# Reordering the first stage, and the last gate pair with its neighbours, in a one-core hybrid decoder step

## The chip, the cores and the metric

The kernel runs on one core of one Trainium2 chip. The metric is the device time of one execution in microseconds. Engine names are those of the profile: PE is TensorE, DVE is VectorE, ACT is ScalarE, POOL is GpSimd, SP is the engine that issues most DMAs. Each engine runs its own instructions strictly in order, and so does SP's queue of DMA issues: what waits for a semaphore holds everything behind it.

## The reference

One layer is computed for a prompt of 1024 tokens with 16 meta tokens ahead of it, and for 8 single sample tokens. All matrices are float32.

```
xn = rmsnorm(h, norm_pre);  proj = xn @ w_in                  # 1024 -> 10 sections of 1024
q, fr, i_in, z_a, b_g, c_g, h_c, z_b, gate_a, gate_b = split(proj)
f = lb + (1 - lb) * sigmoid(fr);  k = 1 - f;  q = silu(q)
o_t = q_t^T S_t,   S_t = diag(f_t) S_{t-1} + k_t v_t^T        # per head, 8 heads of 128 x 128
y_a = (rmsnorm(o) * silu(z_a)) @ w_a
u = c_g * h_c;  y_b = (b_g * conv3(u) * silu(z_b)) @ w_b
out = (sigmoid(gate_a) * y_a + sigmoid(gate_b) * y_b) @ w_o
h = h + rmsnorm(out, norm_post)
```

It also returns the recurrent state and the last two convolution rows for the prompt and the samples.

## The kernel before, in words

Each product of float32 numbers is made of three products of a cheaper type: a value is split into a high part (a cast on ACT) and a low part (value minus high part, a subtraction on DVE or POOL), and `mm3` (lines 114 to 116) multiplies high by high, high by low and low by high. A "product" below is one such PE instruction.

The token axis is cut into two halves of 524 columns (512 prompt tokens and 12 small ones), and each half into two pieces C0 (256 columns) and C1 (268). The program has these stages.

**First stage** (lines 980 to 1126). Eight chunks of 128 tokens are loaded: chunks 0, 2, 4, 6 by SP, chunks 1, 3, 5, 7 by an indirect DMA on POOL (line 167). Their tiles are u, a, s, ee, kt, v, x, zs in that order. For each chunk `square` takes the mean square on ACT (line 176) and its reciprocal root on POOL (lines 82 and 83, tile st), `normalise` scales it on DVE (line 183), `turns` transposes it on PE in two halves of four (line 192), `highs` casts on ACT (line 196) and `lows` subtracts on DVE (line 200). `plain` then multiplies the first two weight tiles, wi (tiles s4h, s4l, into psum ga) and wf (s5h, s5l, into psum gb), with four blocks of the tokens: s0 and s1 are chunks of the first half, s3 and s6 of the second; the weights' parts come from `w_high` on ACT and `w_low`. In all there are 8 such blocks of 24 products. `sums12` (line 219 on DVE, two per chunk pair) and `sums34` (line 219 on POOL) form sums of blocks, and some of these are transposed again: they feed the next stage.

**The Strassen stream.** `strassen` multiplies pairs of weight tiles by the block sums s0 to s6, with 7 instead of 8 block products. A pair has 14 steps: j = 0 to 6, for C0 and C1, with 12 products in each. In each step the weights for two steps later are split (line 605 on ACT, 611 on DVE or POOL), the results of the step before are taken out (`after`; line 570 copies j = 0, 2, 4 into a tile sc on ACT, two buffers; line 288 adds psum and sc on DVE), and then the `hooks` of that step run: a table from step number to side work (`at_step`). A0 is the first step of the pairs that multiply w_a, B0 = A0 + 56 that of w_b. The last pair ahead of A0 is a gate pair, for channels 6 and 7 of gate_b.

**Around A0.** `gate_pair` (line 749) takes a sigmoid of each result piece and stores it, 8 pieces of 128 by 256 or 260, to gb in memory; half of the pieces are stored out of the sc tile itself. `exchange` loads rows of the mixer's output into tiles u, v, a, kt, it (line 877) and splits them into new parts s0 to s6 (ACT line 90, DVE or POOL line 91), in steps A0-13 to A0+9. `block_sums` (line 840) loads two whole rows of the convolution branch, makes four sums of them on DVE (line 219) and stores them (lines 853 to 857): 12 steps each. `gates_in` loads two whole gate tiles of branch A for one pair of y (line 899); `y_pair` multiplies by them on DVE (line 911). `context_out` transposes and stores the convolution context. After the w_b pairs comes the output projection.

Of the kernel before, what the change touches and what calls it, by code (L numbers as in the profile page):

```python
# [20 lines left out]
HY = 516  # L21
# [11 lines left out]
def hybrid_step(ctx: ExitStack, tc: tile.TileContext,  # L33
# [26 lines left out]
    def slot(tag, n=NX, dt=F32):  # L60
        return sb.tile([128, n], dt, name=tag, tag=tag, bufs=BUFS.get(tag, 1))
# [46 lines left out]
    def sec_of(sec, m):  # L108
        c0 = 1024 * sec + 128 * m
        return w_in[0][:, c0:c0 + 128]  # L110
# [35 lines left out]
    def chunks_of(n):  # L146
        return (0, 256), (256, n - 256)
# [55 lines left out]
    def turns(c):  # L203
        for kk in range(2):
            turn(c, kk)
# [78 lines left out]
    def added(pt, s, out=None):  # L284
        if s is None:
            return pt
        out = s if out is None else out
        vec.tensor_tensor(out=out, in0=pt, in1=s, op=ALU.add)  # L288
        return out
# [459 lines left out]

    def gate_pair(sec, m, dst):  # L750
        def evac(r, h, c0, n, pt, s):
            y = added(pt, s)

            def gate():
                out = slot("cs", HL - 256)[:, 0:n] if s is None else s
                sigmoid(y, n, out)
                sync.dma_start(dst[m + r][:, HY * h + c0:HY * h + c0 + n], out)
            then(gate)

        return (sec_of(sec, m), sec_of(sec, m + 1)), chunks_of(HY), (), evac, lambda: None, factors  # L760

# [100 lines left out]
    def at_step(g, f):  # L862
        hooks.setdefault(g, []).append(f)
# [84 lines left out]

    gates = [gate_pair(8, m, ga_d) for m in (0, 2, 4, 6)] + [gate_pair(9, m, gb_d) for m in (0, 2, 4, 6)]
    stream_of = [head_pairs(0)[1]]  # L950
# [11 lines left out]
    exchange(B0 - 26, B0 - 14, sets_b, ob_d, *sums_b, ("kt", "x", "zs"))  # L962
    at_step(A0 + 18, lambda: context_out())

    def at_steps(g, side):
        for i in range(12):
            at_step(g + i, lambda: next(side, None))
# [3 lines left out]
    for k in range(4):  # L971
        at_steps(S0 + int(15.75 * (k + 5)) + 5, block_sums(k, oz_d, *sums_a, ("f", "k", "s")))
        at_steps((A0 - 52, A0 - 40, A0 - 28, A0 + 2)[k], block_sums(k, ob_d, *sums_b, ("f", "k", "s") if k < 3 else ("x", "zs", "x")))
    for i, m in enumerate((0, 2, 4, 6)):
        at_step(A0 - 11 + 14 * i, lambda m=m: gates_in(m))
        at_step(B0 - (4 if i else 11) + 14 * i, lambda m=m: gates_in_b(m))
# [5 lines left out]
    load_chunk(0)  # L982
    load_chunk(1)
    load_chunk(3)
    sync.dma_start(wpre, norm_pre.broadcast_to([128, 1024]))
# [9 lines left out]
    load_chunk(6)  # L995
    load_small()
    wi, wf = (tuple(p[:, 0:1024] for p in t) for t in (t3, t4))
# [4 lines left out]
    def w_low(r, w, kk):  # L1002
        ks = slice(512 * kk, 512 * kk + 512)
        pool.tensor_tensor(out=w[1][:, ks], in0=r[kk], in1=w[0][:, ks].bitcast(F32), op=ALU.subtract)

    def plain(w, h, c0, n):
# [6 lines left out]
        return lambda: (i_out if w is wi else f_out)(0, h, c0, n, pt, None)  # L1013

    square(0)
    load_chunk(5)
    load_chunk(7)
    square(2)
    normalise(0)
    turns(0)  # L1020
    normalise(2)
    highs(0)
    square(1)
    lows(0)
    turns(2)
    for kk in range(2):
        w_high(ri, wi, kk)
        w_low(ri, wi, kk)
    highs(2)
    normalise(1)  # L1030
    lows(2)
    square(3)
    for kk in range(2):
        w_high(rf, wf, kk)
        w_low(rf, wf, kk)
    e1 = plain(wi, 0, *C0)
    turns(1)
    normalise(3)
    highs(1)
    lows(1)  # L1040
    square(4)
    turns(3)
    normalise(4)
    square(6)
    highs(3)
    lows(3)
    e2 = plain(wf, 0, *C0)
    turns(4)
    normalise(6)
    e1()  # L1050
    highs(4)
# [20 lines left out]
    vec.tensor_scalar(out=omlb, in0=lb, scalar1=-1.0, scalar2=1.0, op0=ALU.mult, op1=ALU.add)  # L1072
    square("s", 24)
    e1 = plain(wi, 1, *C0)
    turns(6)
    normalise("s", 24)
    highs(6)
    lows(6)
    square(5)
    square(7)  # L1080
    e2()
    flush()
    e2 = plain(wf, 1, *C0)
    normalise(5)
    s11, s12, s21, s22 = turn_small()
    for b, to in ((s11, b11), (s12, b12), (s21, b21), (s22, b22)):
        small_parts(b, to)
    normalise(7)
    turns(5)
    e1()  # L1090
    highs(5)
    lows(5)
    e1 = plain(wi, 0, *C1)
    turns(7)
    for out, a, b in ((s12, s12, s11), (s22, s22, s12), (s11, s22, s11), (s21, s21, s22)):
        less(out, a, b, vec)
    small_parts(s22, t2)
    e2()
    flush()
    highs(7)  # L1100
    lows(7)
    for i in range(2):
        sums12(i)
    e2 = plain(wf, 0, *C1)
    turn(1, 1)
    turn(3, 1)
    for i in range(2, 4):
        sums12(i)
    next(stream)
    for c in (1, 3):  # L1110
        turn_high(c, 1, t2)
        turn_low(c, 1, t2)
    e1()
    for i in range(4):
        sums34(i)
    e1 = plain(wi, 1, *C1)
    e2()
    flush()
    turn(5, 1)
    turn(7, 1)  # L1120
    e2 = plain(wf, 1, *C1)
    for c in (5, 7):
# [158 lines left out]
```

## Time and profile before

| what | value |
|---|---|
| time, median of 3 runs | 1298.46 us (1297.31 to 1299.75) |
| time of the profiled execution | 1297.85 us |
| its span, first to last instruction | 1296.1 us |
| PE busy | 1242.4 us, 96% of the span |
| DVE busy | 950.1 us, 73% |
| ACT busy | 581.8 us, 45% |
| POOL busy | 458.1 us, 35% |
| moved by DMA | 140.41 MB, mean 108 GB/s |
| mean granted clock of PE | 0.990 |

The time of the profiled execution is 1.75 us more than its span. The page cuts the span into 40 slices of 32.4 us. PE is at 9 tenths or more in nearly all of them; it is at 6 and 8 in the first two, at 8 in the slices from 875, 1004 and 1102 us, and at 7 in the last. So the places where PE waits are few, and they are looked at by stretches of time.

### The profile page before, as it was taken

The page shows a single profiled execution, that of the slowest core. Times are in us where ns is not written, and L with a number is a line of the kernel's source. Part 1 is how long each engine was busy: PE and PEld are TensorE (multiplying, and loading weights), DVE is VectorE, ACT ScalarE, POOL GpSimd, SP SyncE. Part 2 cuts the span into 40 slices and gives each one's busy share as a digit, 9 for nine tenths or more (in the row PEclk, how much of TensorE's full clock was granted, in tenths as well). Part 3 has the DMA queues.
Part 4 walks back from the last instruction along what each step waited for, and adds up shares of the span by engine and source line. Part 5 has one row for each costly group of instructions (what it writes and reads, how often), then busy time and mean ns, then how long its engine had stood idle before and what let it go on. Part 6 is the DMA issues. An engine that isn't in the chain of part 4 may idle for free. (4 is left out here: it accounts for less than half of the span.)

```text
span 1296.1 us, 25464 instructions
## 1 busy us (share of the span) xinstructions
PE 1242.4 (96%) x9849; PEld 1203.3 (93%) x9849; DVE 950.1 (73%) x1572; ACT 581.8 (45%) x1392; POOL 458.1 (35%) x510
## 2 busy tenths in 40 slices
PE   6899999999999999999999999998999899899997
PEld 5799999999999999999999999998999899899876
DVE  5779586785958678595885788688679757979252
ACT  5455555454555545555443333333334535436031
POOL 5734243333423333242433355335434524430010
PEclk9899999999999999999999999999999999999999
DMA  6011212121121212112113434553576746633141
GB/s 223 9 39 59 64 58 83 58 72 56 58 68 58 83 52 74 61 58 68 58 62 105 140 115 122 164 196 116 176 241 232 252 129 217 195 124 116 49 165 57
DMA packets 160199, 140.41 MB, mean 108 GB/s; under 512 B 10097, under 2 KB 134106, under 8 KB 160078
## 3 DMA queue, kind: packets, MB, share of 16 engines
q1 hardware_dynamic: 159502, 136.69, 33.2%
q0 software_dynamic: 576, 2.10, 0.4%
q8 instruction: 77, 1.26, 0.4%
q14 instruction: 44, 0.36, 0.1%
HBM read 104.27 MB, written 34.45 MB: 107 GB/s over the span
## 5 line engine op out<-in xcount | busy, mean ns | idle before, releaser
L611 DVE TENSOR_TENSOR w<-wq,w 128x512 fp32r<-128x512 f32 x185 | 161.3, 872 | 69.5 <-ACT w L605 64.1
L605 ACT CAST w<-sm 128x512 fp32r<-128x512 f32 x141 | 87.3, 619 | 186.3 <-PE gb L116 150.8
L591 POOL TENSOR_TENSOR sm<-wq 128x512 f32<-128x512 f32 x47 | 74.6, 1587 | 197.0 <-DVE w L611 165.3
L615 POOL TENSOR_TENSOR sm<-wq,sm 128x512 f32<-128x512 f32 x47 | 70.5, 1501 | 198.1 <-DVE w L611 161.2
L570 ACT COPY sc<-ga 128x256 f32<-128x256 f32 x216 | 80.0, 372 | 125.4 <-PE ga L116 108.3
L611 DVE TENSOR_TENSOR w<-sm,w 128x512 fp32r<-128x512 f32 x141 | 103.4, 733 | 36.5 <-ACT w L605 36.0
L605 ACT CAST w<-wq 128x512 fp32r<-128x512 f32 x188 | 116.7, 622 | 26.8 <-PE ga L116 18.7
L114 PE MATMUL gb<-s6h,w 128*128 128x256 f32 (+3 forms) x376 | 109.0, 290 | 6.7 <-DVE sc L288 5.8
L116 PE MATMUL gb<-s3h,w 128*128 128x256 f32 (+3 forms) x376 | 108.1, 288 | 5.4 <-DVE w L611 5.3
L114 PE MATMUL gb<-s3h,w 128*128 128x256 f32 (+3 forms) x376 | 109.6, 292 | 2.7 <-DVE sc L288 2.2
L288 DVE TENSOR_TENSOR sc<-gb,sc 128x256 f32<-128x256 f32 x192 | 80.7, 422 | 40.4 <-PE gb L116 26.7
L114 PE MATMUL gb<-s1h,w 128*128 128x256 f32 (+3 forms) x376 | 108.6, 289 | 0.1
L115 PE MATMUL gb<-s6l,w 128*128 128x256 f32 (+3 forms) x376 | 107.5, 286 | 0.0
L115 PE MATMUL gb<-s3l,w 128*128 128x256 f32 (+3 forms) x376 | 107.4, 286 | 0.0
L116 PE MATMUL gb<-s6h,w 128*128 128x256 f32 (+3 forms) x376 | 107.1, 285 | 0.0
L116 PE MATMUL gb<-s1h,w 128*128 128x256 f32 (+3 forms) x376 | 106.2, 283 | 0.5 <-DVE w L611 0.4
L115 PE MATMUL gb<-s1l,w 128*128 128x256 f32 (+3 forms) x376 | 106.2, 282 | 0.0
L593 POOL TENSOR_TENSOR sm<-wq 128x512 f32<-128x512 f32 x47 | 66.2, 1409 | 81.5 <-DVE w L611 78.1
L114 PE MATMUL ga<-s5h,w 128*128 128x256 f32 (+3 forms) x288 | 84.4, 293 | 4.6 <-ACT sc L570 4.1
L114 PE MATMUL ga<-s2h,w 128*128 128x256 f32 (+3 forms) x288 | 84.4, 293 | 0.0
L114 PE MATMUL ga<-s0h,w 128*128 128x256 f32 (+3 forms) x288 | 83.1, 289 | 1.1 <-DVE zs L327 1.1
L114 PE MATMUL ga<-s4h,w 128*128 128x256 f32 (+3 forms) x288 | 82.6, 287 | 0.0
(699 smaller groups left out, 4466.5 us busy)
## 6 DMA issues: line engine op xcount, KB each, us to landing
wq<-in_w_in_dram SPq DMA_DIRECT2D x160, 256.0 KB
oz<-zs SPq DMA_DIRECT2D x16, 258.0 KB
ob<-zs SPq DMA_DIRECT2D x8, 516.0 KB
wq<-in_w_a_dram SPq DMA_DIRECT2D x16, 256.0 KB
wq<-in_w_b_dram SPq DMA_DIRECT2D x16, 256.0 KB
wq<-in_w_o_dram SPq DMA_DIRECT2D x16, 256.0 KB
wq<-in_x_prompt_dram SPq DMA_DIRECT2D x16, 256.0 KB
out_dram<-w SPq DMA_DIRECT2D x16, 256.0 KB
```

Source lines behind the costliest of these rows:

```text
L114: pe.matmul(pt, wh, xh, start=first, stop=False, skip_group_check=onto)
L115: pe.matmul(pt, wh, xl, start=False, stop=False, skip_group_check=onto)
L116: pe.matmul(pt, wl, xh, start=False, stop=last, skip_group_check=onto)
L288: vec.tensor_tensor(out=out, in0=pt, in1=s, op=ALU.add)
L570: act.copy(held[j][:, cols], o)
L591: pool.tensor_tensor(out=s3, in0=a11, in1=a21, op=ALU.subtract)
L593: pool.tensor_tensor(out=s2, in0=a21, in1=a11, op=ALU.subtract)
L605: act.copy(w[:, 0:512], source(i))
L611: (pool if j in pairs[p][2] else vec).tensor_tensor(out=w[:, 512:1024], in0=source(i), in1=w[:, 0:512].bitcast(F32), op=ALU.subtract)
L615: pool.tensor_tensor(out=s2, in0=raws[p, 0, 1], in1=s2, op=ALU.subtract)
```

## The change

The change has two parts.

**First stage.** PE gets 13 products of the identity by itself ahead of the first transposes, and 4 more after those of chunk 2 (`spin`, results unused). The indirect loads of chunks 1 and 3 are issued on POOL after the squares of chunks 0 and 2 instead of first. `w_low` moves from POOL to DVE. The squares, normalisations, casts, the small rows and the sums are put in another order: each `sums12` now stands between the lows of two chunks instead of all four behind them, and the transposes of chunk 3 and of some sums stand behind a block of products instead of ahead of it.

**Around A0.** The last gate pair writes its sigmoids into two whole tiles (tags x and zs) and stores each of them once, two steps after the pair's end. `gates_in` is hooked 5 steps later for each of its four pairs, the last `block_sums` 6 steps later, `context_out` 4 steps later.

```
--- before.py
+++ after.py
@@ -747,17 +747,29 @@
 
         return (sec_of(4, m), sec_of(7, m)), chunks_of(HY), (), evac, end, factors
 
-    def gate_pair(sec, m, dst):
+    def gate_pair(sec, m, dst, whole_=False):
+
+        kept_ = []
+
+        def end():
+            if whole_:
+                later.append(lambda: later.append(lambda: [sync.dma_start(dst[m + r], kept_[r]) for r in range(2)]))
+
         def evac(r, h, c0, n, pt, s):
+            if whole_ and not kept_:
+                kept_.extend((slot("x", NY), slot("zs", NY)))
             y = added(pt, s)
 
             def gate():
+                if whole_:
+                    sigmoid(y, n, kept_[r][:, HY * h + c0:HY * h + c0 + n])
+                    return
                 out = slot("cs", HL - 256)[:, 0:n] if s is None else s
                 sigmoid(y, n, out)
                 sync.dma_start(dst[m + r][:, HY * h + c0:HY * h + c0 + n], out)
             then(gate)
 
-        return (sec_of(sec, m), sec_of(sec, m + 1)), chunks_of(HY), (), evac, lambda: None, factors
+        return (sec_of(sec, m), sec_of(sec, m + 1)), chunks_of(HY), (), evac, end, factors
 
     def context_out():
         for g in range(2):
@@ -946,7 +958,7 @@
             hi, lo = (slot(t, 1024, F32R)[:, 0:1024] for t in ("x", "zs"))
         (merged_parts if which else out_weight)(k, hi, lo)
 
-    gates = [gate_pair(8, m, ga_d) for m in (0, 2, 4, 6)] + [gate_pair(9, m, gb_d) for m in (0, 2, 4, 6)]
+    gates = [gate_pair(8, m, ga_d) for m in (0, 2, 4, 6)] + [gate_pair(9, m, gb_d, m == 6) for m in (0, 2, 4, 6)]
     stream_of = [head_pairs(0)[1]]
     for m in range(1, 8):
         vf, qz_ = head_pairs(m)
@@ -960,7 +972,7 @@
     stream_of += [y_pair(w_b, m, sets_b, True) for m in (0, 2, 4, 6)]
     exchange(A0 - 34, A0 - 14, sets_a, oz_d, *sums_a, ("u", "v", "a", "kt", "it"))
     exchange(B0 - 26, B0 - 14, sets_b, ob_d, *sums_b, ("kt", "x", "zs"))
-    at_step(A0 + 18, lambda: context_out())
+    at_step(A0 + 22, lambda: context_out())
 
     def at_steps(g, side):
         for i in range(12):
@@ -970,9 +982,9 @@
     S0 = 14 * 25
     for k in range(4):
         at_steps(S0 + int(15.75 * (k + 5)) + 5, block_sums(k, oz_d, *sums_a, ("f", "k", "s")))
-        at_steps((A0 - 52, A0 - 40, A0 - 28, A0 + 2)[k], block_sums(k, ob_d, *sums_b, ("f", "k", "s") if k < 3 else ("x", "zs", "x")))
+        at_steps((A0 - 52, A0 - 40, A0 - 28, A0 + 8)[k], block_sums(k, ob_d, *sums_b, ("f", "k", "s") if k < 3 else ("x", "zs", "x")))
     for i, m in enumerate((0, 2, 4, 6)):
-        at_step(A0 - 11 + 14 * i, lambda m=m: gates_in(m))
+        at_step(A0 - 6 + 14 * i, lambda m=m: gates_in(m))
         at_step(B0 - (4 if i else 11) + 14 * i, lambda m=m: gates_in_b(m))
     for k, g in enumerate((3, 6, 9)):
         at_step(B0 + 42 + g, lambda k=k: (out_parts(k, 0), out_parts(k, 1)))
@@ -980,8 +992,6 @@
 
     C0, C1 = chunks_of(HL)
     load_chunk(0)
-    load_chunk(1)
-    load_chunk(3)
     sync.dma_start(wpre, norm_pre.broadcast_to([128, 1024]))
     load_chunk(2)
     ri = [load_quarter(sec_of(2, 0), kk) for kk in range(2)]
@@ -993,7 +1003,6 @@
     rf = [load_quarter(sec_of(1, 0), kk) for kk in range(2)]
     load_chunk(4)
     load_chunk(6)
-    load_small()
     wi, wf = (tuple(p[:, 0:1024] for p in t) for t in (t3, t4))
 
     def w_high(r, w, kk):
@@ -1001,7 +1010,7 @@
 
     def w_low(r, w, kk):
         ks = slice(512 * kk, 512 * kk + 512)
-        pool.tensor_tensor(out=w[1][:, ks], in0=r[kk], in1=w[0][:, ks].bitcast(F32), op=ALU.subtract)
+        vec.tensor_tensor(out=w[1][:, ks], in0=r[kk], in1=w[0][:, ks].bitcast(F32), op=ALU.subtract)
 
     def plain(w, h, c0, n):
 
@@ -1012,42 +1021,57 @@
             mm3(pt, w[0][:, ks], w[1][:, ks], xh[:, c0:c0 + n], xl[:, c0:c0 + n], k == 0, k == 7)
         return lambda: (i_out if w is wi else f_out)(0, h, c0, n, pt, None)
 
+
+    def spin(n):
+        idle = bbank()
+        for _ in range(n):
+            pe.matmul(idle[:, 0:128], ident, ident, start=True, stop=True)
+
+    spin(13)
     square(0)
+    load_chunk(1)
+    square(2)
+    load_chunk(3)
+    normalise(0)
+    turns(0)
+    w_high(ri, wi, 0)
+    normalise(2)
+    highs(0)
+    w_high(ri, wi, 1)
+    lows(0)
+    turns(2)
+    spin(4)
+    w_low(ri, wi, 0)
+    highs(2)
+    w_low(ri, wi, 1)
+    square(1)
+    lows(2)
+    load_small()
     load_chunk(5)
     load_chunk(7)
-    square(2)
-    normalise(0)
-    turns(0)
-    normalise(2)
-    highs(0)
-    square(1)
-    lows(0)
-    turns(2)
-    for kk in range(2):
-        w_high(ri, wi, kk)
-        w_low(ri, wi, kk)
-    highs(2)
     normalise(1)
-    lows(2)
-    square(3)
     for kk in range(2):
         w_high(rf, wf, kk)
+    square(3)
+    e1 = plain(wi, 0, *C0)
+    for kk in range(2):
         w_low(rf, wf, kk)
-    e1 = plain(wi, 0, *C0)
     turns(1)
+    square(4)
+    highs(1)
     normalise(3)
-    highs(1)
     lows(1)
-    square(4)
+    square(6)
+    normalise(4)
+    e2 = plain(wf, 0, *C0)
+    square("s", 24)
     turns(3)
-    normalise(4)
-    square(6)
     highs(3)
     lows(3)
-    e2 = plain(wf, 0, *C0)
+    e1()
+    normalise("s", 24)
+    normalise(6)
     turns(4)
-    normalise(6)
-    e1()
     highs(4)
     lows(4)
     pvp = hbank()
@@ -1070,55 +1094,53 @@
     vec.reciprocal(out=e1, in_=e1)
     vec.tensor_tensor(out=lb, in0=lb, in1=e1, op=ALU.mult)
     vec.tensor_scalar(out=omlb, in0=lb, scalar1=-1.0, scalar2=1.0, op0=ALU.mult, op1=ALU.add)
-    square("s", 24)
     e1 = plain(wi, 1, *C0)
+    square(5)
+    square(7)
     turns(6)
-    normalise("s", 24)
     highs(6)
     lows(6)
-    square(5)
-    square(7)
+    s11, s12, s21, s22 = turn_small()
+    for b, to in ((s11, b11), (s12, b12), (s21, b21), (s22, b22)):
+        small_parts(b, to)
     e2()
     flush()
     e2 = plain(wf, 1, *C0)
     normalise(5)
-    s11, s12, s21, s22 = turn_small()
-    for b, to in ((s11, b11), (s12, b12), (s21, b21), (s22, b22)):
-        small_parts(b, to)
+    sums12(0)
+    e1()
+    e1 = plain(wi, 0, *C1)
+    turns(5)
+    highs(5)
     normalise(7)
-    turns(5)
+    lows(5)
+    e2()
+    flush()
+    turns(7)
+    sums12(1)
+    e2 = plain(wf, 0, *C1)
+    highs(7)
+    lows(7)
+    turn(1, 1)
+    turn(3, 1)
     e1()
-    highs(5)
-    lows(5)
-    e1 = plain(wi, 0, *C1)
-    turns(7)
+    sums12(2)
+    next(stream)
+    e1 = plain(wi, 1, *C1)
+    for c in (1, 3):
+        turn_high(c, 1, t2)
+        turn_low(c, 1, t2)
+    sums12(3)
+    e2()
+    flush()
     for out, a, b in ((s12, s12, s11), (s22, s22, s12), (s11, s22, s11), (s21, s21, s22)):
         less(out, a, b, vec)
     small_parts(s22, t2)
-    e2()
-    flush()
-    highs(7)
-    lows(7)
-    for i in range(2):
-        sums12(i)
-    e2 = plain(wf, 0, *C1)
-    turn(1, 1)
-    turn(3, 1)
-    for i in range(2, 4):
-        sums12(i)
-    next(stream)
-    for c in (1, 3):
-        turn_high(c, 1, t2)
-        turn_low(c, 1, t2)
-    e1()
+    turn(5, 1)
+    e2 = plain(wf, 1, *C1)
     for i in range(4):
         sums34(i)
-    e1 = plain(wi, 1, *C1)
-    e2()
-    flush()
-    turn(5, 1)
     turn(7, 1)
-    e2 = plain(wf, 1, *C1)
     for c in (5, 7):
         turn_high(c, 1, t2)
         turn_low(c, 1, t2)
```

Three pieces of the instruction order show what the diff alone does not. Row names are as in the profile: line, operation, tile written, tiles read, shape; a number behind x counts equal rows.

This is DVE near the start of the program, before (-) and now (+); s is chunk 2, a chunk 1, ee chunk 3, s4l and s5l the low parts of the first two weight tiles:

```order
 L183 SCALAR_TENSOR_TENSOR s<-s,st,x 128x1024
 L200 TENSOR_TENSOR s0l<-h,s0h 128x4x128
 L200 TENSOR_TENSOR s1l<-h,s1h 128x4x128
-L183 SCALAR_TENSOR_TENSOR a<-a,st,x 128x1024
+L1013 TENSOR_TENSOR s4l<-wq,s4h 128x512 x2
 L200 TENSOR_TENSOR s0l<-h,s0h 128x4x128
 L200 TENSOR_TENSOR s1l<-h,s1h 128x4x128
+L183 SCALAR_TENSOR_TENSOR a<-a,st,x 128x1024
+L1013 TENSOR_TENSOR s5l<-wq,s5h 128x512 x2
```

The normalisation of chunk 1 moved behind the second pair of lows, and the weights' lows, which POOL made, stand in its place.

This is DVE later in the first stage, v being chunk 5 and zs chunk 7; a, ee and v in lines 219 are the sums:

```order
+L183 SCALAR_TENSOR_TENSOR v<-v,st,x 128x1024
+L219 TENSOR_TENSOR a<-a,u 128x512
+L219 TENSOR_TENSOR a<-a 128x512
 L183 SCALAR_TENSOR_TENSOR zs<-zs,st,x 128x1024
 L200 TENSOR_TENSOR s3l<-h,s3h 128x4x128
 L200 TENSOR_TENSOR s6l<-h,s6h 128x4x128
+L219 TENSOR_TENSOR ee<-ee,s 128x512
+L219 TENSOR_TENSOR ee<-ee 128x512
+L200 TENSOR_TENSOR s3l<-h,s3h 128x4x128
+L200 TENSOR_TENSOR s6l<-h,s6h 128x4x128
+L219 TENSOR_TENSOR v<-v,kt 128x512
+L219 TENSOR_TENSOR v<-v 128x512
```

The sums were one run of eight behind the lows of chunk 7; now those of chunks 1 and 3 stand ahead of these lows.

This is DVE around step A0+10 before, the last block sums (line 219) among the exchange's lows (line 91), the weights' lows (line 611) and the take-out of results (lines 288 and 911):

```order
L91 TENSOR_TENSOR s6l<-a,s6h 128x516 x2
L219 TENSOR_TENSOR x<-x 128x516
L611 TENSOR_TENSOR w<-sm,w 128x512
L91 TENSOR_TENSOR s6l<-kt,s6h 128x516 x2
L219 TENSOR_TENSOR x<-zs,x 128x516
L288 TENSOR_TENSOR sc<-gb,sc 128x256
```

And the same place now:

```order
L91 TENSOR_TENSOR s6l<-a,s6h 128x516 x2
L611 TENSOR_TENSOR w<-sm,w 128x512
L91 TENSOR_TENSOR s6l<-kt,s6h 128x516 x2
L288 TENSOR_TENSOR sc<-gb,sc 128x256
L923 TENSOR_TENSOR f<-sc,f 128x256
```

Two of the four sums stood ahead of the sc row; all four now stand further on, behind the results of two more steps.

## Rows read from the trace of the kernel before

**Rows 1.** Stretches: length; PE, PEld, DVE, ACT, POOL busy; PEclk; DMA share; GB/s.

```profile
112.00:987.76 875.76, 864.67 (x7243) 854.27 (x7242) 669.12 (x1106) 403.38 (x1003) 323.40 (x378) 1.00 0.31 97
987.76:1040.42 52.66, 44.64 (x339) 44.23 (x338) 42.69 (x63) 29.12 (x63) 23.51 (x16) 0.91 0.69 232
1061.59:1081.72 20.13, 20.13 (x170) 20.13 (x169) 10.45 (x22) 6.29 (x13) 5.41 (x4) 1.00 0.56 184
```

**Rows 2.** What PE waited for in the first 62 us (total, times, longest).

```profile
PE h L192 <- DVE ee L219: 2.7, 1, 2.7
PE ga L115 <- DVE s0l L200: 1.7, 1, 1.7
...
PE h L192 <- DVE v L183: 1.3, 1, 1.3
PE h L192 <- DVE zs L219: 1.2, 1, 1.2
PE h L192 <- DVE a L219: 1.0, 1, 1.0
```

**Rows 3.** PE in order of time: start, duration, instructions, idle before.

```profile
11.53 1.97 PE L192 MATMUL h<-ident,s 128*128 128x128 f32 x8 [1.49 <-DVE s L183]
...
15.65 0.58 PE L115 MATMUL ga<-s0l,s4h 128*128 128x256 f32 x1 [1.70 <-DVE s0l L200]
...
18.16 0.41 PE L114 MATMUL ga<-s1h,s4h 128*128 128x256 f32 x1
...
20.51 1.04 PE L192 MATMUL h<-ident,a 128*128 128x128 f32 x8
...
60.17 0.28 PE L114 MATMUL ga<-s0h,w 128*128 128x256 f32 x1
```

**Rows 4.** Busy time by stretches: the second half of the first stage.

```profile
33.69:45.67 11.98, 10.40 (x72) 9.82 (x72) 8.28 (x18) 8.00 (x23) 3.29 (x4) 0.86 0.00 1
45.67:60.17 14.50, 9.62 (x64) 9.23 (x65) 14.40 (x12) 4.34 (x9) 14.34 (x10) 0.88 0.06 16
```

**Rows 5.** DVE in order of time, first stage.

```profile
12.70 2.29 DVE L183 SCALAR_TENSOR_TENSOR a<-a,st,x 128x1024 f32<-128x1024 f32 x1
14.91 0.68 DVE L200 TENSOR_TENSOR s0l<-h,s0h 128x512 fp32r<-128x512 f32 x1
...
46.44 1.75 DVE L219 TENSOR_TENSOR ee<-ee,s 128x512 f32<-128x512 f32 x1
```

**Rows 6.** POOL in order of time, first stage and after it.

```profile
6.63 1.07 POOL L167 DMA_INDIRECT v<-in_x_prompt_dram,rows_of  x1 [0.19 <-issue]
...
17.05 3.54 POOL L1004 TENSOR_TENSOR s5l<-wq,s5h 128x512 fp32r<-128x512 f32 x2
...
44.48 1.48 POOL L611 TENSOR_TENSOR w<-wq,w 128x512 fp32r<-128x512 f32 x1 [8.29 <-ACT w L605]
...
65.95 1.29 POOL L611 TENSOR_TENSOR w<-wq,w 128x512 fp32r<-128x512 f32 x1
```

**Rows 7.** PE in order of time, early in the stream.

```profile
72.21 0.37 PE L114 MATMUL gb<-s3h,w 128*128 128x256 f32 x1
...
116.84 1.14 PE L440 MATMUL h<-x,u 128*128 128x128 f32 x8
```

**Rows 8.** PE in order of time, around A0.

```profile
1006.03 0.39 PE L114 MATMUL ga<-s5h,w 128*128 128x256 f32 x1 [3.73 <-ACT sc L570]
...
1035.09 0.58 PE L114 MATMUL gb<-s6h,w 128*128 128x256 f32 x1 [4.29 <-DVE sc L288]
```

**Rows 9.** Busy time by stretches, around the two waits of rows 8.

```profile
1002.30:1010.50 8.20, 4.47 (x25) 4.47 (x25) 5.38 (x9) 4.16 (x10) 5.58 (x4) 0.79 0.94 327
...
1030.80:1040.42 9.62, 5.33 (x25) 5.33 (x26) 9.27 (x15) 0.62 (x1) 2.66 (x2) 0.67 0.30 111
```

**Rows 10.** ACT in order of time, ahead of the first wait.

```profile
1005.60 0.37 ACT L570 COPY sc<-ga 128x256 f32<-128x256 f32 x1 [4.25 <-DMA gb<-sc]
```

**Rows 11.** DVE in order of time, ahead of the second wait.

```profile
1034.01 0.68 DVE L219 TENSOR_TENSOR x<-zs,x 128x516 f32<-128x516 f32 x1
```

## The prediction

> **What bounds the kernel.** I read the busy table by stretches first. From 112 to 987.76 us PE is busy 864.67 of 875.76 us [rows 1]: there PE is the bound, and what starts earlier ends earlier by as much. The change touches two places where PE is not full. One is the first stage: the stream's first product starts at 60.17 us [rows 3]. The other is the 28 steps from 987.76 to 1040.42, which take 52.66 us; an undisturbed pair of 14 steps (168 products) takes 20.13, so two would take 40.26, and 12.4 are lost [rows 1]. Then I read the list of waits and PE's timeline in each place, and last the engine that each wait names.
>
> **First stage, what is lost before.** PE's own work from the product at 15.65 to 60.17 is 192 products and 64 transposes. A product costs 20.13/168 = 0.12 us [rows 1], a set of 8 transposes 1.04 [rows 3]; with 0.8 for the small ones (my estimate) that is 23.0 + 8.3 + 0.8 = 32.1 of 44.5 us. So 12.4 are lost, and the rows name them. The first block runs slowly: from 15.65 to the transposes at 20.51 there are 23 products, 4.86 us where 2.76 would do: 2.1 [rows 3]. The wait for v is 1.3, those for the sums ee, a and zs 2.7 + 1.0 + 1.2 = 4.9 [rows 2]. The granted clock is 0.86 over 11.98 us and 0.88 over 14.50; the missing shares, 0.14 x 11.98 and 0.12 x 14.50, are 1.7 + 1.7 [rows 4]. Half a microsecond remains in small waits.
>
> **What the change does to each.**
>
> *Start.* The product at 15.65 waited 1.70 for s0l of chunk 2 [rows 2, 3]. On DVE that subtraction starts at 14.91 behind the normalisation of chunk 1, which took 2.29 [rows 5]. This moves behind it; two weight lows come in its place, 0.68 each if they cost what a sum of that length costs alone [rows 11]. POOL is idle then, since the lows are what it did, 3.54 for two [rows 6]. That gives 2.29 - 1.36 = 0.9. Chunk 2's own normalisation, for which PE waited until 11.53 [rows 3], comes earlier too, because the loads of chunks 1 and 3 no longer run beside chunk 2's. How much, no row shows: between 0, and 1.5, the wait in that row. It also gets an indirect issue of 1.07 on POOL [rows 6] ahead of its reciprocal root. I take 0.9. The first block then starts at 15.65 - 1.8 = 13.8.
>
> A sum of two tiles in SBUF took 1.75 beside POOL's work [rows 5] and 0.68 alone [rows 11]; the two new weight lows on DVE read two such tiles as well. The Trainium skill (GPSIMD Engine Reference, "1. Specifications") says that POOL and DVE share their interfaces to SBUF, so that a DVE instruction with two inputs from SBUF contends. By that rule these lows pay wherever POOL still works beside them: 2 x 1.75 would make the start 2.1 later, and the sum 1285. POOL then has only scalars of one column and indirect issues left, so I keep 0.68.
>
> *The loads.* Chunks 1 and 3 land some microseconds later; behind them ACT's squares wait in order. Their first use on PE is behind a block of 24 products, which hides up to 2.9 us; I cost them at nothing.
>
> *The extra products.* An instruction on the identity is two PE rows (4 products of this kind are x8 in rows 7), a row costs 1.97/8 = 0.25 early on [rows 3]: 26 rows are at most 6.4 us, from about 1.5 on, done at about the time the first transposes can start. They delay nothing. The 4 others, 1.1 to 2.0 us, lie beside the wait for s0l. What they may give is the clock of the first block. In rows 3 the products are slow until about 20 us, after 4 us of unbroken work, though 16 transposes and a product ran before. Now there are products earlier, but between the 13 and the 4 only transposes and waits. I take half: 1.1 of the 2.1 is still lost.
>
> *The wait at C1* (1.3, for v) had small rows and chunk 6 behind it on ACT and DVE. These come earlier, but two squares were moved ahead of chunk 6's casts on ACT; PE is earlier too. I keep 1.6 (the 1.3 and 0.3 of the small waits) and half of the slow clock behind it, 0.9.
>
> *The sums.* A sum took 1.75 [rows 5], beside POOL's sums; alone it is 0.68 [rows 11]. Six of eight now stand ahead of or between the lows, before POOL's start. Only the last pairs still run beside POOL. I keep 1.2 of the 4.9 and nothing of the second clock loss.
>
> Lost after: 1.1 + 1.6 + 0.9 + 1.2 = 4.8. The stream starts at 13.8 + 32.1 + 4.8 = 50.7, 9.5 earlier. Bounds: with nothing more than the start and the clock of the sums' stretch, 1.8 + 1.7 = 3.5; with no loss but half of the wait at C1, 60.17 - (13.8 + 32.1 + 0.8) = 13.5.
>
> **Around A0.** The first wait is 3.73 us for ACT's copy into sc [rows 8], and ACT waited 4.25 us for a gate store to have read that buffer [rows 10]. Whole tiles take this reader away, so the wait goes. The 24 products behind it run at a mean clock of 0.79 over 8.20 us; 4.47 - 24 x 0.12 = 1.6 goes with it [rows 9]. What is late next is DVE: it has 42.69 us of work in a stretch that would be 40.26 long [rows 1]; I give back 0.6. Sum 4.7.
>
> The second wait is 4.29 for DVE's sc [rows 8]; DVE is busy 9.27 of 9.62 us there [rows 9]. Two of the four block sums stood before that row, 0.68 each [rows 11]: 1.4 goes, 2.9 is left, and I leave the slow clock behind it (0.67 over 9.62 us [rows 9]) as it is. Sum 4.7 + 1.4 = 6.1. Bounds: 1, if DVE takes the place of the first wait; 10, if the second wait and its slow products go as well.
>
> The other edits are costed at nothing. The sums go to steps A0+14 to 17, where an undisturbed pair leaves DVE idle for half the time (10.45 of 20.13 [rows 1]). The gates are asked for 10 steps, 14.4 us, before their use instead of 15. Eight gate stores on SP, each waiting for its sigmoid with the exchange's loads queued behind, become two that stand two steps behind the last sigmoid and wait for nothing; behind them stand the loads of kt and a weight. SP's three sum stores now stand among the w_a weights' loads, which have five steps until their use. The tiles x and zs are free: their last readers are the convolution of channel 6. `context_out` meets an idle ACT. If any of these covers fails it is a wait of one or two steps, 1.4 to 2.9 us.
>
> **Sum.** 9.5 + 6.1 = 15.6. From the profiled execution's 1297.85 that is 1282.3; this run lies 0.6 below the median of the runs, so on the median I predict 1283.
>
> **Rivals.**
>
> *The first stage's gain is given back in the stream.* POOL works from 44.48 to 67.24 without a pause on sums and weight lows, and its low at 65.95 is needed by the product at 72.21, 12.0 behind the stream's start [rows 3, 6, 7]. Now POOL can start about 3 us earlier, and PE 9.5. With the same 22.8 of work it ends at 64.3, and the product wants it at 62.7: 1.6 lost, and more if ACT's cast comes later. Against it: beside fewer DVE sums POOL's own would be shorter. If it costs 4 to 5 with the clock behind it: 1287.5. 0.17.
>
> *The wait at sc is only exchanged.* DVE's 42.69 in 40.26 speaks for it. Gain 9.5 + 1: 1288. 0.10.
>
> *The gates come late, and the kernel is slower.* 14.4 us between asking and use decide: DMA share is 0.94 between 1002 and 1010 [rows 9], and a store there held ACT for 4.25 [rows 10]. A late gate stops DVE in order at line 911, and with it the weights' lows and PE, in each of four pairs. To lose the 15.6 and 2.6 more, a landing must take 14.4 + 4.5 = 19 us in all four. Only the first pair lies in the crowded stretch, so this is improbable: 1301, 0.04.
>
> *Nothing moves on balance*: the loads of chunks 1 and 3 land so late that ACT, in order, holds the first stage back by 9, and DVE keeps the loss at A0; 1297, 0.03.
>
> **Numbers.** My forecast has 0.66; 0.17 + 0.10 are slower forms of it that are still faster than before. A measurement can tell about 0.2%, 2.6 us, from no change. So faster 0.93, same 0.03, slower 0.04. The range goes down to the better bounds taken half way, 1298.5 - 22 = 1276, and up past the first two rivals to 1291.
>
> **What would show it.** In the profile after: the stream's first ga product near 50.7 instead of 60.17; its first counted product near 13.8; sums of line 219 on DVE at 0.7 rather than 1.75; the stretch around A0 at 46 to 47 us instead of 52.66, with no ACT wait for a gb store, and a DVE sc wait of about 3 left at step A0+12; the stretch from 112 on shifted and otherwise unchanged. I am wrong if the stream starts after 56, if PE waits for POOL's lows early in the stream, or if the stretch around A0 stays above 50.

## The result, and the profile after

The changed kernel takes 1284.39 us (median of 4 runs, 1283.49 to 1285.15); the kernel before, on the same chip, 1299.11 (4 runs). The ratio is 0.9888 [0.9871, 0.9905]. The profiled execution takes 1284.25 us with a span of 1282.5, 13.6 less than before. Marks in PE's timeline split these 13.6; each is the start of the same product in both kernels.

| from, to | before | after | difference |
|---|---|---|---|
| start to the stream's first product | 60.17 | 49.78 | -10.4 |
| from there to the last group (j = 6) of the second pair | 50.81 | 52.90 | +2.1 |
| from there to the gate pair of channels 6 and 7 | 876.78 | 876.81 | 0.0 |
| the 28 steps around A0 | 52.66 | 47.13 | -5.5 |
| from there to the end | 255.68 | 255.88 | +0.2 |

The stretches by engine, with the columns of [rows 1] (the first runs from C1's first product to the stream; the fourth answers to the second of [rows 1], the last to the third):

```profile
33.33:49.78 16.45, 16.06 (x128) 15.46 (x129) 16.14 (x23) 9.09 (x20) 7.95 (x5) 1.00 0.01 2
49.78:102.68 52.90, 47.87 (x386) 45.66 (x384) 46.79 (x70) 27.18 (x64) 30.09 (x34) 1.00 0.15 42
102.68:979.49 876.81, 866.02 (x7249) 855.53 (x7250) 667.68 (x1108) 404.15 (x1005) 324.33 (x378) 1.00 0.31 97
979.49:1026.62 47.13, 42.90 (x339) 42.01 (x337) 41.24 (x58) 28.73 (x63) 23.92 (x16) 0.96 0.72 242
1047.58:1067.71 20.13, 20.13 (x170) 20.13 (x169) 11.12 (x22) 6.29 (x13) 5.19 (x4) 1.00 0.60 190
```

In the first one PE is busy 16.06 of 16.45 us, at a granted clock of 1.00. The same 128 products and transposes took 24.57 us in the kernel before, busy 19.41, at 0.86:

```profile
35.60:60.17 24.57, 19.41 (x128) 18.52 (x129) 20.91 (x27) 10.46 (x29) 16.10 (x11) 0.86 0.03 9
```

What PE still waits for in the first 62 us (total, times, longest) answers to [rows 2]. Of the waits for sums (line 219), one of 0.2 is left. The longest wait, 2.4 for s, is no loss against before: the transposes of chunk 0 end earlier, and those of chunk 2 start at 11.39 (11.53 before).

```profile
PE h L192 <- DVE s L183: 2.4, 1, 2.4
...
PE h L192 <- DVE kt L183: 1.3, 1, 1.3
...
PE ga L114 <- ACT it L306: 1.0, 1, 1.0
PE ga L115 <- DVE s0l L200: 0.9, 1, 0.9
...
PE h L192 <- DVE ee L183: 0.5, 1, 0.5
...
PE h L192 <- DVE zs L219: 0.2, 1, 0.2
```

PE in order of time (as [rows 3]): the extra products, the first counted product (the one that waits for s0l, second of its block), the end of its block, the stream's first product, and the first wait behind it.

```profile
1.46 5.41 PE L1028 MATMUL gb<-ident 128*128 128x128 f32 x26 [1.46 <-POOL ident masks.py:199]
...
14.39 0.39 PE L115 MATMUL ga<-s0l,s4h 128*128 128x256 f32 x1 [0.89 <-DVE s0l L200]
...
17.22 1.03 PE L192 MATMUL h<-ident,a 128*128 128x128 f32 x8
...
49.78 0.36 PE L114 MATMUL ga<-s0h,w 128*128 128x256 f32 x1
...
53.29 0.39 PE L114 MATMUL ga<-s0h,w 128*128 128x260 f32 x1 [0.96 <-ACT it L306]
```

The 2.1 given back early in the stream are DVE's. Four subtractions of 128 x 48, 0.81 us for all four in the kernel before, now stand where POOL forms its eight sums. First their row before; then, in the changed kernel, DVE by shape, 49 to 60 us (busy, mean ns), POOL beside it in order of time, and ACT, which needs their result and waited 7.30 for it with the copy `it` behind:

```profile
39.83 0.81 DVE L219 TENSOR_TENSOR cs<-cs 128x48 f32<-128x48 f32 x4
```

```profile
L219 DVE TENSOR_TENSOR cs<-cs 128x48 f32<-128x48 f32 x4 | 5.0, 1257 | 0.1
...
L200 DVE TENSOR_TENSOR s2l<-h,s2h 128x512 fp32r<-128x512 f32 x2 | 1.3, 676 | 0.0
```

```profile
48.66 1.74 POOL L219 TENSOR_TENSOR u<-a,u 128x512 f32<-128x512 f32 x1
50.36 1.29 POOL L219 TENSOR_TENSOR u<-u,a 128x512 f32<-128x512 f32 x1
51.62 1.26 POOL L219 TENSOR_TENSOR s<-ee,s 128x512 f32<-128x512 f32 x1
```

```profile
51.76 0.23 ACT L90 CAST s2h<-cs 128x48 fp32r<-128x48 f32 x1 [7.30 <-DVE cs L219]
```

Each of these 128 x 48 operations takes as long as one of POOL's, 1.26, some six times its own 0.20; an operation of DVE with one input in PSUM (h) and ten times the columns takes 0.68 among them. The Trainium skill (SBUF — State Buffer, "SBUF: two separate sides") says that a VectorE operation with two SBUF inputs and a GpSimd operation that reads SBUF exclude each other for the whole instruction. These rows agree: POOL's sums read SBUF. PE's waits that come of DVE's delay are the 0.96 at 53.29, 0.42 at 59.22, and at the second pair's last group 1.55 in place of 0.95.

Around A0, PE's waits (as [rows 8]) are now four short ones in place of 3.73 and 4.29:

```profile
995.28 0.39 PE L116 MATMUL ga<-s5h,w 128*128 128x256 f32 x1 [1.01 <-DVE w L611]
...
1011.01 0.36 PE L114 MATMUL gb<-s3h,w 128*128 128x256 f32 x1 [1.33 <-DVE sc L288]
1011.98 0.39 PE L116 MATMUL gb<-s3h,w 128*128 128x256 f32 x1 [0.50 <-DVE w L611]
...
1023.65 0.39 PE L114 MATMUL gb<-s6h,w 128*128 128x256 f32 x1 [1.40 <-DVE sc L288]
```

All four name DVE; no wait of ACT for a store of gb is left ([rows 10] had 4.25).

### The profile page after: what moved, and what is told of

It reads as the page before. It is cut to its first block, busy times and chain, and to the rows that moved or that the text cites. A ratio compares the mean times of both kernels' runs of the same rounds, so it can differ in the third digit from the quotient of the medians.

```text
span 1282.5 us, 25517 instructions
## 1 busy us (share of the span) xinstructions
PE 1240.3 (97%) x9883; PEld 1200.5 (94%) x9883; DVE 954.6 (74%) x1576; ACT 580.3 (45%) x1392; POOL 454.8 (35%) x506
## 3 DMA queue, kind: packets, MB, share of 16 engines
q8 instruction: 77, 1.26, 0.4%
```

## Experiments

The changed kernel's median differs by 3.3 us between its two measurements (below), so smaller effects are read from the profile, by the marks of the table.

**Each part alone.** One kernel has only the first-stage edits, one only those around A0 (the diff above, split in two).

> The kernel before with the first-stage part of the change alone. Theory (the two parts are independent, and the first stage is worth what the gate pair of channel 7 comes earlier in the profile after, 987.76 - 979.49 = 8.3 us): stream's first ga product at 49.8, gate pair 7 at 979.5, and the stretch of 28 steps behind it as before, 52.7; median 1299.1 - 8.3 = 1290.8. Rival (the part around A0 gains only because the stream comes earlier against the transfers): then the stretch falls under 50 here too, and the median is under 1288.

> The kernel before with the part around A0 alone (gate pair in whole tiles, and the three other step numbers). Theory: stream's first product at 60.2 and gate pair 7 at 987.8 as before, the stretch of 28 steps 47.1 instead of 52.7; median 1299.1 - 5.3 = 1293.8. Rival (the two parts need each other): the stretch stays above 50, median above 1296.5.

First stage alone: 1292.16 us, ratio 0.9951 [0.9935, 0.9967]; stream at 50.57, gate pair at 978.96, stretch 52.82 with waits of 4.01 and 4.28. Part around A0 alone: 1291.78 us, 0.9957 [0.9940, 0.9973]; stream at 60.78, stretch 47.05. Each stretch has its change's value without the other part: the theory holds, both rivals fall. By medians the parts are worth 6.3 and 6.7, 12.9 together, against 14.7 for the whole change in its own measurement. The two medians missed the expected ones by 1.4 and 2.0, inside their intervals; the split into 8.3 and 5.5 rests on the marks.

**Whole tiles alone, steps alone.** The part around A0, split again: `gate_pair(9, m, gb_d, m == 6)` with the old step numbers, and the new step numbers without it.

> The kernel before with the last gate pair in whole tiles, but with the old step numbers for the last block sums, the gates and context_out. Theory (the prediction's split of the gain around A0): the 4.0 us wait for ACT's sc and the slow products behind it go, the wait for DVE's sc in front of the step A0+12 stays at 4.3 with its slow products; the stretch of 28 steps takes 47.5 to 48.5 instead of 52.7. Rival (the store was only the last of several, and DVE holds the same place): an equally long wait on DVE's w or sc near the first place, stretch above 50.5.

> The kernel before with only the step numbers changed (last block sums at A0+8, gates at A0-6, context_out at A0+22), the gate pair stored in pieces as before. Theory: the 4 us wait for ACT's sc behind a gate store stays; the wait for DVE's sc at A0+12 falls from 4.3 to between 1.4 and 2.9, and the stretch takes 50 to 51.3. Rival (the gates' loads, asked for at A0-11, are what kept the gate stores back on SP's queue): the first wait falls under 2 as well, and the stretch under 49.

Whole tiles: stretch 47.80 (1292.29 us, 0.9958 [0.9939, 0.9976]). Steps: 49.64 (1293.81 us, 0.9966 [0.9953, 0.9979]). So 4.9 and 3.0 alone, 5.6 together: they overlap. With the whole tiles alone the size is as expected, but the wait for DVE's sc at A0+12 did not stay at 4.3, though the sums stand where they stood:

```profile
1029.51 0.39 PE L114 MATMUL gb<-s6h,w 128*128 128x256 f32 x1 [0.49 <-DVE sc L288]
...
1032.63 0.39 PE L114 MATMUL gb<-s6h,w 128*128 128x260 f32 x1 [1.41 <-DVE sc L288]
```

So more than half of the second wait goes with the whole tiles as well, and new waits for DVE in earlier steps (0.35, 1.40, 0.50) take a part back. With the steps alone PE's waits are:

```profile
1002.54 0.39 PE L114 MATMUL ga<-s5h,w 128*128 128x256 f32 x1 [0.82 <-ACT sc L570]
...
1019.30 0.36 PE L114 MATMUL gb<-s3h,w 128*128 128x256 f32 x1 [1.66 <-DVE sc L288]
...
1032.33 0.39 PE L114 MATMUL gb<-s6h,w 128*128 128x256 f32 x1 [3.43 <-DVE sc L288]
```

My theory for this kernel failed on the first wait: it falls from 3.73 to 0.82 though the stores are as before. ACT's waits for gb's stores are 4.0 in all, as 4.5 before, but the longest is 1.6 and no longer 4.25. So gate stores were held up by what was moved away from them. Of the three things moved, only the gates' loads, from A0-11 to A0-6, stand ahead of that wait at A0-4; the sums and the context stand behind it, at A0+2 and A0+18 even in the kernel before. So the rival is right about the cause, though the stretch (49.64) stayed above its 49. SP's issues, the kernel before and then this one (ee is the first gate tile, sc the gate piece whose store ACT waits for):

```profile
995.50 0.60 SPq L899 DMA_DIRECT2D ee<-ga  x1
...
999.30 0.44 SPq L757 DMA_DIRECT2D gb<-sc  x1
```

```profile
997.45 0.41 SPq L757 DMA_DIRECT2D gb<-sc  x1
...
1001.58 0.42 SPq L899 DMA_DIRECT2D ee<-ga  x1
```

ACT goes on at 1005.60 before and at 1002.11 here, 2.9 earlier counted from the stretch's start (987.76 and 987.18): the store is issued 1.3 earlier, and ACT has its buffer 4.7 after the issue instead of 6.3. With the whole tiles alone the first wait goes too, and all that PE still waits for is DVE: from about 47 us on DVE bounds this stretch.

**No extra products.** The two lines `spin(13)` and `spin(4)` are gone.

> The changed kernel without the 17 extra products on the identity. Theory (they keep TensorE's clock up for the first block): the first counted product still at 14.4, but its block takes 4.9 us as in the kernel before instead of 3.0, and of these 1.9 up to 1.3 are taken up by the wait for chunk 4's tile at 23.95 (1.33 now), so the stream starts 0.6 to 1.9 later, 50.4 to 51.7; median 1285 to 1286.3. Rival (the first block is fast because of what else moved, and the extra products do nothing): block 3.0, stream at 49.8, median 1284.4 as after.

The first counted product is at 14.41; its block reaches to 19.21, 4.8 instead of 2.83; the stream starts at 51.60; 1286.05 us, 0.9904 [0.9890, 0.9918]. On the block the theory holds. PE in order of time, second half of the block:

```profile
17.99 0.41 PE L116 MATMUL ga<-s1h,s4l 128*128 128x256 f32 x1
18.20 0.41 PE L114 MATMUL ga<-s1h,s4h 128*128 128x256 f32 x1
...
18.74 0.28 PE L114 MATMUL ga<-s1h,s4h 128*128 128x256 f32 x1
18.86 0.28 PE L115 MATMUL ga<-s1l,s4h 128*128 128x256 f32 x1
```

Products start 0.21 us apart, then 0.12. In the eight profiles that have the extra products and this order of loads, the block ends between 17.2 and 18.7 us, 0.5 to 2.0 earlier. In some of these the extra products themselves are slow and end after s0l is there: the first counted product then starts up to 0.7 late (15.18 where s0l was done at 14.43). The granted clock of the slow stretch does not show the slow products; it reads 1.00:

```profile
13.20:18.50 5.30, 4.67 (x21) 4.38 (x21) 2.47 (x4) 3.17 (x6) 1.36 (x3) 1.00 1.10 326
```

The later stream is not shown to come from this. In this profile chunk 1 also landed late (see below): DVE normalised it at 17.78, and PE could not have gone on before 19.2 with a faster block either. The kernel with the sums in one run, further on, has the extra products, and in its profile chunk 1 was normalised at 17.78 too. The first product of C1 there, and then in the kernel without extra products:

```profile
35.14 0.39 PE L114 MATMUL ga<-s0h,s4h 128*128 128x268 f32 x1 [0.27 <-ACT s0h L90]
```

```profile
35.13 0.39 PE L114 MATMUL ga<-s0h,s4h 128*128 128x268 f32 x1 [0.25 <-ACT s0h L90]
```

So the stream came 1.8 later, as expected, but chunk 1 alone accounts for it. What the extra products are worth where chunk 1 is on time, no run shows; the changed kernel was not measured beside this one, and its two medians, 1284.39 and 1287.65, lie on both sides.

**Loads first.**

```diff
     load_chunk(0)
+    load_chunk(1)
+    load_chunk(3)
     sync.dma_start(wpre, ...)
...
     square(0)
-    load_chunk(1)
     square(2)
-    load_chunk(3)
```

> The changed kernel with the loads of chunks 1 and 3 issued directly behind that of chunk 0, as in the kernel before. The prediction's step (these loads beside chunk 2's delay it by 0.9): normalisation of chunk 2 at 10.9 instead of 10.05, first counted product at 15.3, stream 0.9 later. Rival (what the profile after suggests: chunk 2's normalisation moved by only 0.14, so these loads do not delay it): normalisation of chunk 2 within 0.2 of 10.05, stream within 0.5 of 49.8, median as after.

Chunk 2 is normalised at 10.11, against 10.05: my step was wrong, these loads do not delay it. They delay a weight instead. ACT in order of time, this kernel and then the changed one:

```profile
11.22 0.62 ACT L1011 CAST s4h<-wq 128x512 fp32r<-128x512 f32 x1 [2.11 <-DMA wq<-in_w_in_dram]
```

```profile
8.94 0.60 ACT L1009 CAST s4h<-wq 128x512 fp32r<-128x512 f32 x1
```

The first counted product is at 15.50, 1.1 later, but the stream starts at 50.16: the wait for ee (0.46 in the changed kernel) is gone and the one at C1 is 0.26 instead of 0.58, while the wait for kt is 1.33 in both. 1284.99 us, 0.9895 [0.9871, 0.9920].

**The eight sums in one run.**

```diff
-    sums12(0)
...
-    sums12(3)
...
     lows(7)
+    for i in range(4):
+        sums12(i)
     turn(1, 1)
```

> The changed kernel with VectorE's eight 128x512 sums (line 219) in one run behind the lows of chunk 7, where POOL works without a pause. Theory (a VectorE operation with two SBUF inputs waits for POOL's operation in progress): they take 1.3 to 1.7 us each instead of 0.68, some 12 us in all, PE waits for a, ee, v and zs again 4 to 5 us in all instead of 0.2, and the stream starts 4 to 6 us later, 54 to 56; median 1288 to 1290. Rival (the sums were slow before only because the data came late or for a cause that the change took away): 0.68 each, 5.4 in all, stream at 50 to 51.

DVE in order of time:

```profile
42.88 0.68 DVE L219 TENSOR_TENSOR a<-a,u 128x512 f32<-128x512 f32 x1
43.59 1.75 DVE L219 TENSOR_TENSOR a<-a 128x512 f32<-128x512 f32 x1
45.26 1.75 DVE L219 TENSOR_TENSOR ee<-ee,s 128x512 f32<-128x512 f32 x1
...
53.79 1.68 DVE L219 TENSOR_TENSOR zs<-zs 128x512 f32<-128x512 f32 x1
```

POOL's first operation starts at 43.53; the sum ahead of that takes 0.68, all seven behind it 1.63 to 1.77. PE waits 2.07 and 2.43, and its granted clock falls:

```profile
43.41:57.70 14.29, 9.79 (x65) 9.44 (x65) 14.15 (x11) 2.13 (x5) 14.01 (x9) 0.76 0.00 1
```

The stream starts at 57.70, 7.9 later; 1291.86 us, 0.9959 [0.9945, 0.9972]. The theory holds. Of the 7.9, 1.4 are there before this stretch (chunk 1 came late, see below). The stretch itself takes 6.5 more: 4.3 for the waits (4.5 against 0.2), and the remaining 2.2, which I had left out, lie in slow products.

**The small subtractions early**, and then also the fourth low of the first pair on VectorE.

```diff
     sums12(1)
+    for out, a, b in ((s12, s12, s11), (s22, s22, s12), (s11, s22, s11), (s21, s21, s22)):
+        less(out, a, b, vec)
     e2 = plain(wf, 0, *C1)
     highs(7)
     lows(7)
+    small_parts(s22, t2)
...
     flush()
-    for out, a, b in ((s12, s12, s11), (s22, s22, s12), (s11, s22, s11), (s21, s21, s22)):
-        less(out, a, b, vec)
-    small_parts(s22, t2)
```

The second kernel has besides:

```diff
-            return (tuple(sec_of(x, m) for x in secs), chunks_of(n), () if m else (1, 3, 5),
+            return (tuple(sec_of(x, m) for x in secs), chunks_of(n), () if m else (1, 5),
```

> The changed kernel with the four small subtractions (line 219, 128x48) moved from behind POOL's start of its eight sums to ahead of the casts of chunk 7, and the two halves that follow from them behind those. Theory (a VectorE operation with two SBUF inputs pays for POOL's work beside it): the four take 0.2 us each instead of 1.26, ACT's wait of 7.3 for them and PE's wait of 0.96 at 53.29 go, and of the 2.1 us that the stream gives back in its first steps 1.4 to 2 come back: median 1282.4 to 1283. Rival (what holds DVE there is POOL's other sums and the weight lows behind them): the four are short, but PE waits for the next of DVE's results instead, median 1284.4 within 0.5.

> The changed kernel with the four small subtractions early (as in the experiment before) and with the fourth weight low of the first pair (source 3) on VectorE instead of POOL. Theory (in that experiment POOL's low, 1.2 us late for PE at 64.6, took back half of what the small subtractions gave): PE waits neither for ACT's it at 53 nor for POOL's low; counted from the stream's first product, the step 102.7 of the kernel after comes 1.5 to 2 us earlier; median 1 to 2 us under the changed kernel on this chip. Rival (VectorE, now with one more two-input operation beside POOL, hands the wait on): another wait of 1 us for DVE's w or f, no gain, within 0.5 of the changed kernel.

First kernel: 1287.04 us, 0.9913 [0.9899, 0.9926]. The four take 0.81 together, the wait at 53 is gone, and still the gain missed the forecast: from the stream's first product to the second pair's last group it is 52.30 against 52.90. A wait of 1.20 for POOL takes most of it back, and the four now delay the last sum, for which PE waits 1.02 instead of 0.17:

```profile
64.63 0.39 PE L116 MATMUL gb<-s3h,w 128*128 128x256 f32 x1 [1.20 <-POOL w L611]
```

Second kernel: that wait is gone as well, the distance is 51.55, 1.35 of the 2.1 won back, and the last sum is 1.0 late as before: 0.5 net, by profile. The wait for f at the last group stays, 1.57. 1285.85 us, 0.9903 [0.9887, 0.9918], beside 1287.65 for the changed kernel on the same chip; the ranges overlap.

**The changed kernel again.**

> The changed kernel once more, on the same chip as the three below, so that they are compared with it. Both theories: median 1283.5 to 1286, stream at 49.5 to 50.6 in the profile, the stretch of 28 steps around A0 at 47.1.

1287.65 us (1285.16 to 1289.64), 0.9920 [0.9906, 0.9934], above what I expected; stretch around A0 47.04, but the stream at 52.24. The 2.5 us come from chunk 1. DVE, POOL and ACT in order of time, first in the changed kernel's first profile, then in this one:

```profile
6.54 1.30 DVE L183 SCALAR_TENSOR_TENSOR u<-u,st,x 128x1024 f32<-128x1024 f32 x1 [6.54 <-DMA x<-in_norm_pre_dram]
...
6.59 1.25 POOL L167 DMA_INDIRECT a<-in_x_prompt_dram,rows_of  x1 [0.21 <-issue]
...
13.05 1.07 ACT L176 ACTIVATE zs<-a 128x1024 f32<-128x1024 f32 x1
```

```profile
6.78 1.28 DVE L183 SCALAR_TENSOR_TENSOR u<-u,st,x 128x1024 f32<-128x1024 f32 x1 [6.78 <-POOL st L83]
...
6.95 2.23 POOL L167 DMA_INDIRECT a<-in_x_prompt_dram,rows_of  x1 [0.21 <-issue]
...
16.26 1.06 ACT L176 ACTIVATE zs<-a 128x1024 f32<-128x1024 f32 x1 [2.48 <-DMA a<-in_x_prompt_dram,rows_of]
```

In all nine profiles with this order the indirect issue took 1.25 where it began within 0.07 us of DVE's normalisation (4 profiles) and 2.23 to 2.28 where it began 0.13 to 0.17 behind it (5); in each of these five ACT then waited 1.1 to 3.3 for chunk 1, in none of the four. The other indirect issues sort the same way: in the changed kernel's first profile those of chunks 3 and 5 began 0.16 and 0.15 behind a normalisation and took 2.08 and 2.09, that of chunk 7 began while DVE was idle and took 0.94. The longer issue is not all of it. From issue to landing chunk 1 took 6.0 to 6.1 in the four profiles and 8.3 to 9.6 in the five, so the landing is 2.2 to 3.6 later and the issue only 1.0 longer; where the rest comes from is open. The Trainium skill (SBUF — State Buffer, same section) says that a VectorE operation in a mode that takes two ports keeps GpSimd from writing the descriptors of a DMA that it issues; whether a normalisation, with two inputs from SBUF, is of this kind, no run shows. No run separated the two operations on purpose either, so the cause is argued, not shown.

**All splits of the exchanges on VectorE**, and this together with the small subtractions early and the fourth low on VectorE.

```diff
-                split(r, sets[j][0][:, o:o + HY], sets[j][1][:, o:o + HY], pool if v % 3 == 2 else vec)
+                split(r, sets[j][0][:, o:o + HY], sets[j][1][:, o:o + HY], vec)
```

> The changed kernel with the splits of the two exchanges (line 91) all on VectorE, none on POOL: 16 of 56 move. Theory (a two-input operation of VectorE waits for POOL's in progress, so POOL's help costs VectorE more than it saves: 16 x 0.65 = 10.4 us more work against about 16 waits of 1 us): VectorE's busy time over the two stretches around A0 and B0 falls or stays, 41.2 and 44.0 now, the waits of PE there shrink from 4.2 and 4.2 to under 2.5 each; median 2 to 4 us under the changed kernel. Rival (POOL relieves VectorE, as it is meant to): VectorE's busy time rises by 3 to 5 in each stretch, PE waits longer, median 3 to 8 us above it.

> The two edits of the kernels above together (small subtractions early with the fourth low on VectorE, and all exchange splits on VectorE). They lie 900 us apart, so their effects should add: by the theories of both 3 to 6 us under the changed kernel, 1279 to 1281.5; by the rivals of both 3 to 8 us above it.

1281.50 us (1279.96 to 1282.11), 0.9875 [0.9860, 0.9890], and both together 1280.11 (1279.05 to 1280.94), 0.9861 [0.9845, 0.9876]: 6.2 and 7.5 under the changed kernel on that chip, and every run of theirs under every run of it in both measurements. The stretches around A0 and around B0:

```profile
980.14:1024.91 44.77, 41.05 (x339) 40.43 (x337) 42.33 (x66) 28.70 (x63) 12.32 (x8) 1.00 0.75 255
...
1088.43:1133.73 45.30, 41.80 (x338) 40.67 (x337) 41.76 (x76) 19.46 (x39) 11.72 (x8) 1.00 0.55 176
```

They were 47.13 and 47.49. With 8 more operations, 5.2 us of work, DVE is busy 42.33 in the first one, 1.1 more; in the second, with 3 more (4 moved, and another falls ahead of the mark), 41.76 where it was 43.96. So the rival falls: of what POOL took off DVE it cost most again in longer operations in the first stretch, and more than that in the second. One detail missed: around A0 PE still waits 0.57, 1.59 and 1.56, 3.7 and not under 2.5, and around B0 3.6; more of the gain is that its products are no longer slow (around A0 busy 41.05 against 42.90, clock 1.00 against 0.96). The last kernel's 1.4 under the one before it is within their ranges. These two are the fastest kernels here.

## Why the prediction was right

The time (1283 against 1284.39), the size of both parts (9.5 and 6.1 against 10.4 and 5.5) and their places were right. So was the main mechanism: sums away from POOL's work, and gate stores out of ACT's way. Several terms behind these sizes were not. By its steps:

- *Start, 13.8*: it was 14.39. The first half held (the normalisation of chunk 1 out of the way, two lows at 0.64 each in its place; the price of 1.75 was not paid). The second half was wrong: 0.9 for chunk 2 came out as 0.14; the run with the loads first shows that these loads do not delay it.
- *The loads, at nothing*: right in the first profile, wrong in five of nine; there PE waits 0 to 1.9 for chunk 1. This is the step whose cover was thinnest: the stream of the same kernel starts at 49.8 or at 52.2 by it.
- *Extra products, half of 2.1*: the first block ends 2.0 earlier in the first profile and 0.5 to 2.0 in all, but no run shows what that is worth at the stream. "They delay nothing" was wrong: up to 0.7 at the first counted product. I called it the clock; the granted clock's column does not show it.
- *Wait at C1, 1.6 + 0.9 left*: 0.58 is left there and no clock loss behind it (1.00 from 33.33 on); kt and ee, further ahead, wait 1.33 and 0.46.
- *The sums, 4.9 to 1.2, no clock loss*: 0.17 is left. In the kernel that has them in one run they cost 6.5 again.
- *Lost after, 4.8*: 49.78 - 14.39 - 32.1 = 3.3.
- *Around A0, 6.1*: 5.5. The 4.7 for the whole tiles is 4.9 alone, but by luck: the whole tiles also took more than half of the second wait, which the sum had left to the block sums and to DVE, and 2.25 of new waits took a part back. The first wait was put down to the stores out of sc alone; the steps alone took it from 3.73 to 0.82, because the gates' loads were queued ahead of a store. The second wait fell to 1.40, not 2.9, but DVE's lateness came up six steps earlier, 1.33 + 0.50 at A0+6, with slow products behind it. The two edits overlap by 2.3, which the sum did not see.
- *Rival "given back in the stream"*: not its mechanism, but half its size. POOL's lows were on time; DVE was late beside POOL's sums, 2.1. When DVE's delay was taken out, POOL's low did turn up, 1.20.
- *Rivals at A0*: the gates were never late; the exchanged wait is there as 4.2 us of small ones.

The total was nearer than its terms: +0.9 (first stage), -2.1 (stream) and -0.6 (A0) partly cancel, and that is luck. The second measurement, 1287.65, is as the first rival had it (1287.5), so the time alone does not tell the two apart; the marks do.

## What to carry to other kernels

Before moving a DVE operation with two SBUF inputs, read what POOL does at its new place; where POOL works without a pause, price it at POOL's operation, not at its own length. The smallest ones lose most. Moving work from DVE to POOL can raise DVE's busy time (43.96 against 41.76 around B0). Where an edit is costed at nothing because something hides it, ask how late it may come, and look at more than one profile. An experiment's profile can have a delay of its own (chunk 1 without the extra products): compare it with one that has the same delay.

## What was not expected of the hardware

- A DVE subtraction of 128 x 48 takes 0.20 us alone and 1.26 beside POOL; one of 128 x 512 takes 0.68 and 1.63 to 1.77.
- The same indirect DMA issue takes 1.25 or 2.23 us, sorted by 0.1 us in its start against a DVE operation, and its data land 6.0 to 6.1 or 8.3 to 9.6 us after it.
- Without the extra products, early products run 0.21 us apart at a granted clock that reads 1.00, and 0.12 from about 18.6 us on.
